# Rank and scatter: the first eight tile loads issued whole in place of two halves

## The chip, the cores and the metric

The kernel runs on one core of a Trainium2 chip. The metric is the time of one execution on the device in microseconds, lower being better. The core has five engines with instruction streams of their own: PE (TensorE), DVE (VectorE), ACT (ScalarE), POOL (GpSimd) and SP (SyncE). SP, ACT and POOL issue DMAs, which run on the core's 16 DMA engines. In the profile each issuing engine has a queue of its own: q0 is POOL's, q1 is SP's and q10 is ACT's.

## What is computed

```python
B, N, D = x.shape                      # 8, 2048, 2560, float32
order = np.argsort(scores, axis=1)
ranks = np.argsort(order, axis=1)
out[b_idx, ranks, :] = x
```

Each of the 8 batches has 2048 rows of 2560 floats (10,240 bytes) and one score per row. A row's place in the output is the rank of its score among the 2048 scores of its batch. So 16,384 rows, 168 MB, are read and written once, each at a place that is known only when the scores have been compared.

## The kernel before

A batch is cut into eight groups of 256 rows (`GROUPS`). In a group each of the 128 partitions holds two neighbouring rows, m = 2, so one partition's part of a group is 20,480 contiguous bytes of `x`.

**Ranks (DVE, PE).** For each batch PE spreads the scores to all partitions and DVE counts, column by column, how many scores are smaller (L238). Of batch 0 the groups' ranks come out in four steps (`STEPS`: group 0, 1, 2 to 3, 4 to 7), of the later batches all at once. The ranks are cast to integers in `rank_i` (L276, and L284 for the groups in `THIN`).

**Bulk path (POOL).** `BULK` lists all groups but group 0 of batches 0 to 5, 58 groups in all. Each is loaded into one of eight buffers `x0` to `x7` (`NBUF`) and sent out by two indirect DMAs, the scatters (L422). A scatter takes one of the two rows of each partition, 128 rows of 10,240 bytes, to the places in `rank_i`. Load 0 is issued by SP, loads 1 to 7 by POOL at once behind its set-up. From then on, POOL issues load k + 4 before it scatters group k, once the scatters of group k - 4 have landed (`LAG`). Before the scatters of group k, POOL waits for the whole of load k and for the group's ranks.

**How a load is cut.** `load` (L126) issues one DMA for a group, or, for the groups whose number is in `HALVED`, one DMA per row of a partition. A half has 128 pieces of 10,240 bytes, a whole load 128 pieces of 20,480. `HALVED` is `range(8)`: the first load of each of the eight buffers. `loaded` counts 16 semaphore steps per DMA, so the wait asks for both halves.

**Row copies (SP, ACT).** Group 0 of batches 0 to 5 (`DIRECT`) does not pass through SBUF. SP copies its first 128 rows and ACT the other 128 straight from HBM to HBM, one DMA of 10,240 bytes per row, in loops that load 16 offsets at a time (L390 to L402). They start a batch when DVE has written its byte offsets into `rows_i` (L324). In group 4 of batches 1 to 7 (`THIN`), the scatters skip partitions 48 to 51 (their ranks are pushed out of bounds by `hole`, L284), and those eight rows go as row copies too (L376), by SP for the first, third, fifth and seventh of these groups and by ACT for the others. SP thus issues 800 row copies, ACT 792. Each is split into 16 pieces of 640 bytes, one for each DMA engine.

**End.** SP and ACT wait for all their row copies, SP for the last scatters of all buffers.

Of the kernel before, what the change touches and what calls it, by code (L numbers as in the profile page):

```python
# [40 lines left out]
def kernel(  # L41
# [25 lines left out]
    THIN = [(b, 4) for b in range(1, B)]  # L67
    HOLES = range(48, 48 + 4)

    HALVED = range(8)  # L70

    STEPS = [(0, 1), (1, 2), (2, 4), (4, 8)]

# [28 lines left out]
    with tc.tile_critical(no_gpsimd_drain=True):  # L102
# [17 lines left out]
        def load(line, k, sem):  # L120
            b, g = BULK[k]
            r, m = GROUPS[g]
            rows = x[b, r:r + P * m, :].rearrange("(p j) d -> p (j d)", j=m)
            for j in range(m if k in HALVED else 1):
                part = slice(j * D, (j + 1) * D) if k in HALVED else slice(0, m * D)
                line.eng.dma_start(  # L126
                    out=xb[k % NBUF][:, part], in_=rows[:, part]
                ).then_inc(sem, 16)
                if k:
                    n_load[k % NBUF] += 1  # L130
# [3 lines left out]
        load(sp, 0, s_first)  # L134
        loaded = {0: (s_first, 16 * (2 if 0 in HALVED else 1))}

# [343 lines left out]
```

## Time and profile before

| What | Value |
|---|---|
| Median of 9 runs | 782.57 us (781.41 to 784.08) |
| Profiled execution, time | 783.25 us |
| Profiled execution, span from first to last instruction | 781.5 us |
| DVE busy | 400.1 us (51%) |
| POOL busy | 150.1 us (19%) |
| PE busy | 36.7 us (5%) |
| HBM read, written | 168.41 MB, 168.35 MB (431 GB/s over the span) |
| POOL's loads (L126) | 64: 50 whole, 14 halves, mean 562 ns |
| POOL's scatters (L422) | 116, mean 969 ns |

A span line counts what an engine executes, a DMA issue on POOL included. The DMA share is the mean busy share of the 16 DMA engines; the records of overlapping packets can bring it a little over 1. In a timeline line the first two numbers are the start and the duration in us, then come the engine (SPq and ACTq are the issuing sequencers of SP and ACT), the line, the operation, what is written and read, how many were merged, and in brackets the idle time before it with what ended it. In a line of waits there are the total in us, the number of waits and the longest. In a line of a stretch, the window and its length are followed by busy time and count on PE, PE's weight loads, DVE, ACT and POOL, then the granted PE clock, the DMA share and GB/s. In a line of a DMA queue there are packets, MB and the share of the 16 engines' span.

The trace also has a record of every DMA packet: its queue, size, start and duration. One packet is one contiguous piece that one DMA engine moves; the 4-byte packets are completion signals.

### The profile page before, as it was taken

How to read it: one execution, taken by the hardware profiler on the slowest of the kernel's cores; microseconds unless marked ns; L12 is line 12 of the kernel's file. 1: busy time of each engine (PE TensorE's matmuls, PEld its weight loads, DVE VectorE, ACT ScalarE, POOL GpSimd, SP SyncE). 2: the span in 40 equal slices, each digit the busy share in tenths (PEclk: the TensorE clock that was granted, in tenths of full speed). 3: DMA queues.
4: the chain of work that ended last, by engine and by line, in shares of the span. 5: the costliest groups of instructions: out<-in, count | busy, mean ns of one | idle time of the engine just before them, and what ended most of it. 6: DMA issues, size and time to landing. Idle time of an engine off the chain costs nothing.

```text
span 781.5 us, 8177 instructions
## 1 busy us (share of the span) xinstructions
PE 36.7 (5%) x170; PEld 31.0 (4%) x170; DVE 400.1 (51%) x825; ACT 0.0 (0%) x1; POOL 150.1 (19%) x189
## 2 busy tenths in 40 slices
PE   4000020020020020120000000000000000000000
PEld 4000010010010010120000000000000000000000
DVE  5999979979979979889999200000000000000000
ACT  0000000000000000000000000000000000000000
POOL 4113122212121212112211211121212121220100
PEclk9655555555555555555555555555555555555555
DMA  8999999999999999999999999999999999999995
GB/s 359 419 421 419 422 415 423 417 421 417 424 416 422 417 424 417 421 419 421 419 423 418 421 421 424 417 421 419 423 421 420 421 423 419 419 422 420 418 415 68
DMA packets 77186, 320.15 MB, mean 410 GB/s; under 512 B 28448, under 2 KB 53920, under 8 KB 53920
## 3 DMA queue, kind: packets, MB, share of 16 engines
q0 software_dynamic: 25920, 300.90, 90.5%
q1 hardware_dynamic: 25904, 10.93, 5.5%
q10 hardware_dynamic: 25344, 8.16, 4.6%
q14 instruction: 17, 0.14, 0.0%
q8 instruction: 1, 0.02, 0.0%
HBM read 168.41 MB, written 168.35 MB: 431 GB/s over the span
## 4 chain that ended last, share of the span: by engine, by line
DMA 44%; DVE 25%; another core or an unknown queue 14%; POOL 5%; issue 5%; PE 2%; POOLq 0%; SPq 0%
DMA out_dram<-x,rank_i 38%; DVE trash L238 23%; DMA x<-in_x_dram 6%; POOL out_dram L422 4%; PE ps_all L196 1%; DVE s_all L339 1%; POOL x L126 1%; DMA s_in<-in_scores_dram 0%; PE ps_row L298 0%; PE ps_col L175 0%; POOLq L446 0%; DVE rank_i L276 0%; DVE rank L270 0%; DVE rank L264 0%
## 5 line engine op out<-in xcount | busy, mean ns | idle before, releaser
L238 DVE TENSOR_SCALAR_CACHE_REDUCE trash<-s_all,s_col 128x1792 bf16<-128x1792 f32 (+7 forms) x240 | 315.2, 1349 | 4.6
L422 POOL DMA_INDIRECT out_dram<-x,rank_i x116 | 112.4, 969 | 142.4 <-DMA x<-in_x_dram 36.4
L126 POOL DMA_DIRECT2D x<-in_x_dram x64 | 35.8, 562 | 445.6 <-DMA out_dram<-x,rank_i 425.5
L238 DVE SCALAR_TENSOR_TENSOR trash<-s_all,s_col,mask 128x256 bf16<-128x256 f32 x128 | 61.6, 482 | 0.0
L196 PE MATMUL ps_all<-ident,s_col 128*128 128x128 f32 x128 | 29.1, 420 | 3.1 <-DVE s_all L339 2.8
L196 PEld LDWEIGHTS ps_all<-ident,s_col 128*128 128x128 f32 x128 | 27.1, 228 | 4.3 <-DVE s_all L339 3.3
L298 PE MATMUL ps_row<-ident,rank 128*1 128x128 f32 x26 | 7.9, 405 | 392.3 <-DVE rank_i L284 334.8
L339 DVE COPY s_all<-ps_all 128x512 f32<-128x512 f32 x32 | 20.2, 685 | 1.7 <-PE ps_all L196 1.4
L238 DVE DVE_READ_ACCUMULATOR trash<-s_all,s_col 128x1 f32 x240 | 20.0, 83 | 0.0
L298 PEld LDWEIGHTS ps_row<-ident,rank 128*1 128x1 f32 x26 | 2.0, 98 | 396.4 <-DVE rank_i L284 337.6
L238 DVE DVE_READ_ACCUMULATOR trash<-s_all,s_col,mask 128x1 f32 x128 | 10.7, 84 | 0.0
L309 DVE TENSOR_SCALAR thin_i<-ps_row 1x8 int32<-1x8 f32 x7 | 1.1, 153 | 18.5 <-PE ps_row L298 18.5
L324 DVE TENSOR_SCALAR rows_i<-ps_row 1x256 int32<-1x256 f32 x6 | 2.5, 411 | 4.1 <-PE ps_row L298 4.1
L183 DVE COPY s_col<-ps_col 128x128 f32<-128x128 f32 x1 | 0.3, 293 | 4.6 <-PE ps_col L175 4.6
L276 DVE CAST rank_i<-rank 128x16 int32<-128x16 f32 (+3 forms) x11 | 2.1, 193 | 0.4
L175 PE MATMUL ps_col<-ident,s_in 8*128 8x8 f32 x16 | 2.1, 262 | 3.7 <-DMA s_in<-in_scores_dram 3.7
L175 PEld LDWEIGHTS ps_col<-ident,s_in 8*128 8x128 f32 x16 | 2.0, 210 | 3.7 <-DMA s_in<-in_scores_dram 3.7
L270 DVE TENSOR_TENSOR rank<-rank,acc 128x16 f32<-128x16 f32 (+3 forms) x11 | 1.9, 171 | 0.4
L264 DVE TENSOR_TENSOR rank<-acc,acc 128x16 f32<-128x16 f32 (+3 forms) x11 | 1.9, 170 | 0.4
L284 DVE TENSOR_SCALAR rank_i<-rank,hole 128x2 int32<-128x2 f32 x7 | 1.6, 229 | 0.2
L156 POOL TENSOR_SCALAR_AFFINE_SELECT mask<-mask 128x256 f32<-128x256 f32 x2 | 0.8, 401 | 0.0
L168 DVE MEMSET acc<- 128x128 f32 x1 | 0.2, 165 | 1.1 <-SPq L102 1.1
(10 smaller groups left out, 1.8 us busy)
## 6 DMA issues: line engine op xcount, KB each, us to landing
x<-in_x_dram POOLq DMA_DIRECT2D x50, 2560.0 KB
x<-in_x_dram POOLq DMA_DIRECT2D x14, 1280.0 KB
out_dram<-in_x_dram SPq DMA_DIRECT2D x800, 10.0 KB
out_dram<-in_x_dram ACTq DMA_DIRECT2D x792, 10.0 KB
x<-in_x_dram SPq DMA_DIRECT2D x2, 1280.0 KB, 9.0
out_dram<-x,rank_i POOLq DMA_INDIRECT x116, 48.5
s_in<-in_scores_dram SPq DMA_DIRECT2D x1, 64.0 KB
```

The lines of the kernel that those rows point to most:

```text
L126: line.eng.dma_start(out=xb[k % NBUF][:, part], in_=rows[:, part]).then_inc(sem, 16)
L175: nc.tensor.transpose(out=ps_col[:, B * c:B * (c + 1)], in_=s_in[:, r + j:r + m * P:m], identity=ident[:B, :B],)
L196: nc.tensor.transpose(out=ps_all[:, P * c:P * (c + 1)], in_=s_col[:, c, b:b + 1].to_broadcast([P, P]), identity=ident[:],)
L238: do(out=trash[i][:, :P * (hi_c - lo_c)], in0=s_all[:, P * lo_c:P * hi_c], accum_out=acc[i][:, col:col + 1], **how,)
L264: nc.vector.tensor_tensor(out=rank[:, cols], in0=acc[0][:, cols], in1=acc[1][:, cols], op=OP.add)
L270: nc.vector.tensor_tensor(out=rank[:, cols], in0=rank[:, cols], in1=acc[2][:, cols], op=OP.add)
L276: nc.vector.tensor_copy(out=rank_i[:, cols], in_=rank[:, cols])
L284: nc.vector.tensor_scalar(out=rank_i[:, cols], in0=rank[:, cols], scalar1=hole[:], scalar2=None, op0=OP.add,)
L298: nc.tensor.transpose(out=ps_row[:1, P * j:P * (j + 1)], in_=rank[:, col:col + 1], identity=ident[:],)
L324: nc.vector.tensor_scalar(out=rows_i[b][:].rearrange("o (p j) -> o p j", p=P), in0=ps_row[:1, :WIDE].rearrange("o (j p) -> o p j", p=P), s ...
L339: nc.vector.tensor_copy(out=s_all[:, 512 * q:512 * (q + 1)], in_=ps_all[:, 512 * q:512 * (q + 1)],)
L422: nc.gpsimd.indirect_dma_start(out=out_flat, out_offset=bass.IndirectOffsetOnAxis(ap=rank_i[:, col:col + 1], axis=0), in_=xb[k % NBUF][:, ...
```

## The change

`HALVED` becomes empty. The first load of each of the eight buffers is issued as one DMA of 2,560 KB with 128 pieces of 20,480 bytes, as the other 50 loads already are. SP issues one DMA less, POOL seven less; the waits on these loads count 16 in place of 32. On POOL and SP the order of everything else stays, and the instructions of PE, DVE and ACT are the same.

```diff
     THIN = [(b, 4) for b in range(1, B)]
     HOLES = range(48, 48 + 4)
 
-    HALVED = range(8)
+    HALVED = range(0)
 
     STEPS = [(0, 1), (1, 2), (2, 4), (4, 8)]
```

The function that reads it:

```python
for j in range(m if k in HALVED else 1):
    part = slice(j * D, (j + 1) * D) if k in HALVED else slice(0, m * D)
    line.eng.dma_start(
        out=xb[k % NBUF][:, part], in_=rows[:, part]
    ).then_inc(sem, 16)
```

## The prediction

> **What bounds the kernel now.** I read the row of DMA shares first. Then the stretches, the waits of SP and POOL, the first issues, and last the tail.
>
> ```profile
> DMA  8999999999999999999999999999999999999995
> q0 software_dynamic: 25920, 300.90, 90.5%
> q1 hardware_dynamic: 25904, 10.93, 5.5%
> q10 hardware_dynamic: 25344, 8.16, 4.6%
> ...
> SPq L390 <- DVE rows_i L324: 15.6, 1, 15.6
> ```
>
> The 16 DMA engines are full in 38 of 40 slices. q0 (what POOL issues: tile loads and scatters) takes 90.5% of them. q1 and q10 carry the row copies of SP and ACT. So an issue or a semaphore matters only if it leaves the engines empty or reorders the end.
>
> ```profile
> 1.50 0.83 SPq L126 DMA_DIRECT2D x<-in_x_dram  x2
> 2.69 7.53 POOL L126 DMA_DIRECT2D x<-in_x_dram  x14
> 25.21 1.00 POOL L422 DMA_INDIRECT out_dram<-x,rank_i  x1 [15.00 <-DVE rank_i L276]
> ```
>
> These are all issues of the loads that the edit touches (start, duration). POOL then waits 15.0 us for a rank, SP 15.6 us for the row offsets of batch 0.
>
> ```profile
> 10.00:20.00 10.00, 3.15 (x16) 3.07 (x16) 9.11 (x16) 0.00 (x0) 0.21 (x1) 1.00 1.01 429
> 23.60:54.80 31.20, 0.00 (x0) 0.00 (x0) 30.60 (x71) 0.00 (x0) 5.82 (x6) 0.51 1.03 419
> 54.80:80.50 25.70, 0.00 (x0) 0.00 (x0) 25.32 (x49) 0.00 (x0) 9.44 (x11) 0.50 1.02 420
> 740.00:760.00 20.00, 0.00 (x0) 0.00 (x0) 0.00 (x0) 0.00 (x0) 0.00 (x0) 0.50 1.03 415
> 764.00:770.00 6.00, 0.00 (x0) 0.00 (x0) 0.00 (x0) 0.00 (x0) 0.00 (x0) 0.50 1.05 100
> ```
>
> The last two columns are DMA share and GB/s. There is no gap to win up to 760 us. The tail is the one poor stretch: 764 to 770 is busy at 100 GB/s. In the records of single DMA packets, q0's last packet ends at 769.7 us, q10's at 774.9 and q1's at 777.1. So row copies end the kernel, after the scatters.
>
> ```profile
> 754.07 5.17 ACTq L376 DMA_DIRECT2D out_dram<-in_x_dram  x8
> 755.85 11.47 SPq L376 DMA_DIRECT2D out_dram<-in_x_dram  x16
> ```
>
> SP issues its last row copies until 767.3 us, ACT until 759.2. Whatever delays the row copies is paid behind these lines.
>
> **The change part by part.** *Issues.* SP has one issue less (0.83 / 2 = 0.42 us). POOL has seven less: 7.53 / 14 = 0.54 us each, 3.8 us. Both then wait as before (15.0 and 15.6 us), which hides the gain; without that cover it would be 3.8 us. Nothing is moved past anything else, no wait is added, and the wait for a buffer still asks for its whole tile.
>
> Nor do the engines starve earlier. x0 reaches all 16 engines by 3.4 us and lasts until q0's first packet at 6.8 us, by the packet records. Its packets hold the same bytes in the same order.
>
> The Trainium skill, "DMA: Bandwidth & Descriptors", section "Anatomy of one DMA", fits one DMA as about 2.0 us fixed plus its bytes. Paid one after the other, eight DMAs less would be an estimated 16 us; the share of 1.01 from 10 to 20 us speaks against it.
>
> *Packets.* A half load moves packets of 10240 B, one per partition, a whole load packets of 20480 B. Mean duration by the packet records is 0.386 us for 10240 B and 0.762 us for 20480 B (300 to 700 us). Two halves cost 0.772, so 0.010 us is saved per partition. Seven POOL loads are 7 x 8 = 56 partitions per engine: 0.56 us. The eighth load, x0, is all start-up (0.427 us per packet), and I give it nothing. Seven completion packets of 0.009 us add 0.06 us. Sum: **-0.6 us** on every engine, bounds 0 and -0.7.
>
> *Row copies.* Each is 16 packets of 640 B, one per engine, with a completion packet behind each (0.032 + 0.009 = 0.041 us of one engine). I counted packets per engine by stretch, taking the two row queues as a mean:
> - 23.6 us (first row copy) to 54.7 (last half-load packet): 74.7 q0 packets, 34.4 row copies, 0.46 per packet.
> - 54.7 to 80.4 (scatters alone): 63.0 and 24.6, 0.39.
> - 80.4 to 160: 145.3 (a third of them 20480 B) and 79.8, 0.55.
> - 160 to 740: 0.564. 740 to 760 (scatters alone): 0.569.
>
> So a row ring with work gets about 0.565 copies through per q0 packet, whatever that packet's size. Halving the number of packets in the first stretch halves what it can carry: 37.3 x 0.565 = 21.1. From 82 to 86 us, all 20480 B, the ratio was lower, 0.48; that would give 17.9.
>
> In before that stretch was not at this limit but at the issue's. SP's issues there take 0.52 us with 0.22 between them and 2.5 us more after each 16 (the offsets are loaded again): 16 in 14.3 us, 1.1 per us, 34 in 31 us.
>
> After therefore leaves 34.4 - 21.1 = 13.3 copies per queue behind. Issued copies not yet moved go from about 5 to 18 in each ring. Before stands at 32 from 500 us on, so no issue is blocked. The engine time that the two queues don't use, 26.6 x 0.041 = 1.1 us, goes to the loads, so they end at 54.7 - 0.6 - 1.1 = 53.0 us.
>
> Then the rows catch up. Scatters alone can carry 63.0 x 0.565 = 35.6 copies, and before moved 24.6: 11.0 to spare, 2.3 left behind. From 80.4 to 160: 145.3 x 0.565 = 82.1 against 79.8, again 2.3 to spare. I take **0 to 1** copy per queue as left at 160 us, after which there is no slack. Bulk work gives back nearly all of its 1.1 us here, because the late copies use it.
>
> Bounds: 0 (all caught up) and 16.5 (lower ratio, nothing caught up). I stay near 0 because the spare is larger than the debt in rows of this same trace.
>
> *Price of a copy left behind.* With the scatters nearly gone (764 to 768 us), each row queue moves 2.85 copies per us. One more per queue is 1 / 2.85 = 0.35 us of tail, less 2 x 0.041 that the bulk gained: 0.27 us. One copy: **+0.3 us**.
>
> The Trainium skill, same page, section "Queues, rings and completion order", says that an engine takes turns between its queues packet by packet, a packet being some 9 to 17 descriptors. The turns agree with the rows. But if a copy's two packets went in one turn, the ratio would be 1 instead of the 0.565 measured, the first stretch would carry 37 and nothing would fall behind; the sum would be -0.6.
>
> **Sum.** -0.6 + 0.3 = -0.3 us. The profiled execution took 783.25 us (span 781.5 and 1.75 around it), so 782.95. It stands 0.68 above the median of 782.57, so about **782.3** for the median. A measurement of this kernel tells some 0.2% (1.6 us) from no change, and this is well inside.
>
> **Rivals.** *Slower: the row copies never catch up.* Place: 54.7 to 80.4 us. The 0.39 there need not be lack of issued work. SP's issues last 0.8 to 1.0 us at 66 to 78 us although only 2 to 4 copies per ring are outstanding on average. If one late engine, or the queue itself, holds them back there, the 11.0 spare does not exist. Then 13.3 - 2.3 = 11 stay behind: 11 x 0.27 - 0.6 = +2.4 us, 785.0. With 16.5 it is +3.9, 786.5. It decides from about 8 copies (8 x 0.27 - 0.6 = 1.6). For it: copies end the kernel, and nothing after 160 us has slack. Against it: 740 to 760 us has the same scatters alone and 0.569.
>
> *Faster: a descriptor costs the slowest engine more than the mean.* The completions of one scatter spread over 1.9 us at 68 us and over 7.2 us at the end (763.0 to 770.2). So one engine runs late, and it sets the last scatter. The scatters leave out 56 rows of four partitions; were all on that engine, 56 x 0.387 = 21.7 us were taken off it. Its handicap would be about 28 us in all. Spread over its 1437 data packets of q0, 56 packets less are 3.9% or 1.1 us. With the 0.6 that is -1.7 us, 780.9. Against it: the packet durations scarcely vary (0.385 to 0.388 in nearly every stretch).
>
> *The engines empty at the start* because whole loads are generated later: POOL's first issue took 0.71 us, the others about 0.53, and the later whole loads take 0.57. A delay of that size is covered by x0, so it is 0 here, and I give it no chance of its own.
>
> **How the numbers follow.** Catching up: 0.42, time 782.3, own range 781.0 to 784.0 (runs of before went from 781.4 to 784.1). Never catching up: 0.36, around 785. Slow engine relieved: 0.22, around 781. The range goes from 780.3 (the fast case less half a microsecond of scatter) to 785.9 (between the two prices of the slow case). Faster 0.22, within 0.2% 0.42, slower 0.36.
>
> **What would show it.** q0 down to 25920 - 7 x 144 = 24912 packets and POOL's L126 to 57. POOL's first loads done at about 6.5 us. About 21 row copies per queue moved when the first whole loads end near 53 us, against 33 and 36, and the gap nearly gone by 80 us. SP's last issue within a microsecond of 767.3, and q1's end likewise of 777.1. I am wrong if at 160 us the row queues are still over 8 copies behind, if the tail past q0's last packet is longer than 7.4 us by more than a microsecond, or if the loads leave the engines idle before 20 us.

## The result and the profile after

After takes 784.5 us (median of 21 runs, 783.72 to 792.14; all but one at or below 785.01) against 782.56 us (63 runs, 781.36 to 784.08): 1.0029 times as long, interval 1.0022 to 1.0036. That is slower by 1.9 us, clear of the 0.2% that I had set as the limit.

The page after, its row of DMA shares and its queues:

```profile
DMA  8999999999999999999999999999999999999995
q0 software_dynamic: 24912, 300.90, 90.3%
q1 hardware_dynamic: 25760, 10.93, 5.8%
q10 hardware_dynamic: 25344, 8.16, 4.3%
```

The edit did what it says: q0 has 25920 - 7 x 144 = 24912 packets and the same bytes. The engines are as full as before. The issues after, from the timelines of POOL, ACT and SP:

```profile
2.68 3.87 POOL L126 DMA_DIRECT2D x<-in_x_dram  x7
25.41 1.00 POOL L422 DMA_INDIRECT out_dram<-x,rank_i  x1 [18.87 <-DVE rank_i L276]
...
756.99 5.25 ACTq L376 DMA_DIRECT2D out_dram<-in_x_dram  x8
...
757.12 10.99 SPq L376 DMA_DIRECT2D out_dram<-in_x_dram  x16
```

POOL is done with the loads at 6.6 us and waits 18.9 us in place of 15.0: the saved issues are all given to that wait. ACT's last row copies are issued until 762.2 us in place of 759.2, SP's until 768.1 in place of 767.3. The end of after in stretches (last columns: DMA share, GB/s):

```profile
740.00:760.00 20.00, 0.00 (x0) 0.00 (x0) 0.00 (x0) 0.00 (x0) 0.00 (x0) 0.50 1.03 417
764.00:770.00 6.00, 0.00 (x0) 0.00 (x0) 0.00 (x0) 0.00 (x0) 0.00 (x0) 0.50 1.05 91
770.00:776.00 6.00, 0.00 (x0) 0.00 (x0) 0.00 (x0) 0.00 (x0) 0.00 (x0) 0.50 0.38 19
```

From 740 to 760 us the two are alike (415 GB/s in before). Then after moves 91 GB/s where before had 100, and the engines are still 38% busy from 770 to 776 us. The same last stretch of before:

```profile
770.00:776.00 6.00, 0.00 (x0) 0.00 (x0) 0.00 (x0) 0.00 (x0) 0.00 (x0) 0.50 0.32 17
```

So the whole loss lies behind the scatters, in the row copies. The rest of this text counts them in the packet records: how many rows the two row queues together have moved by a given time. The counts of every profiled execution, in us and rows:

```
kernel (first loads)           rows moved by          last packet    this
                           54    80   160    740     q0   row copy   execution
before (0-7 in halves)   67.0 117.6 277.7 1473.8   769.7    777.1    783.25
before, second profile   71.8 128.0 286.3 1481.8   770.5    776.0    782.13
after (all whole)        42.9 110.9 274.8 1471.2   769.5    778.2    784.29
after, second profile    42.6 111.0 276.1 1471.6   770.3    779.0    785.13
only load 0 whole        71.1 124.7 284.8 1480.2   770.3    776.8    782.91
loads 0-2 whole          71.0 119.2 280.6 1476.8   770.5    777.2    783.37
loads 3-7 whole          42.6 111.3 276.4 1473.0   769.2    777.9    784.00
loads 1-7 whole          42.4 111.1 275.8 1471.5   769.7    778.4    784.53
8-15 in halves instead   42.4 110.7 287.0 1485.4   770.4    775.3    781.39
row copies from 37 us    30.9  69.9 230.5 1428.3   767.9    787.6    791.85
row copies from 61 us     0.0  14.1 170.2 1369.6   766.3    813.5    817.09
first 24 in halves       71.0 128.0 298.8 1514.1   770.6    770.9    778.12
first 32 in halves       72.4 126.7 297.6 1530.6   770.8    766.6    775.21
all 58 in halves         71.6 125.2 294.0 1592.0   771.9    736.8    777.61
```

### The profile page after: what moved, and what is told of

Read it like the earlier page. It is cut to its first block, busy times and chain, and to the rows that moved or that the text cites. A ratio compares the mean times of both kernels' runs of the same rounds, so it can differ in the third digit from the quotient of the medians.

```text
span 782.6 us, 8169 instructions
## 1 busy us (share of the span) xinstructions
PE 36.7 (5%) x170; PEld 31.0 (4%) x170; DVE 400.0 (51%) x825; ACT 0.0 (0%) x1; POOL 146.6 (19%) x182
## 3 DMA queue, kind: packets, MB, share of 16 engines
q0 software_dynamic: 24912, 300.90, 90.3%
## 4 chain that ended last, share of the span: by engine, by line
DMA 50%; another core or an unknown queue 19%; DVE 13%; POOL 7%; issue 6%; PE 1%; POOLq 0%; SPq 0%
DMA out_dram<-x,rank_i 43%; DVE trash L238 12%; DMA x<-in_x_dram 6%; POOL out_dram L422 5%; POOL x L126 1%; PE ps_all L196 0%; DVE s_all L339 0%; DMA s_in<-in_scores_dram 0%; PE ps_col L175 0%; POOLq L446 0%; DVE rank_i L276 0%; DVE rank L270 0%; DVE rank L264 0%; PE ps_row L298 0%
## 5 line engine op out<-in xcount | busy, mean ns | idle before, releaser
L126 POOL DMA_DIRECT2D x<-in_x_dram x57 | 32.1, 563 | 446.0 <-DMA out_dram<-x,rank_i 404.0
```

Source lines behind the costliest of these rows:

```text
L126: line.eng.dma_start(out=xb[k % NBUF][:, part], in_=rows[:, part]).then_inc(sem, 16)
```

## The experiments

Each was timed in five rounds beside before on the same chip; ratios are to before. A kernel's debt is the number of row copies by which it lies behind before at the same time. The row-debt theory says that whole loads make the kernel slower only by this debt: rows that are late stay late, and end the kernel later.

### Which loads count

`e1_x0_whole`:

```diff
-    HALVED = range(8)
+    HALVED = range(1, 8)
```

> Only load 0 (SP's) is issued whole, loads 1 to 7 stay in halves. Row-debt theory (whole loads slow the row copies only while these run, from 23.6 us on): load 0 has landed by then, so 782.6 us, as before. Start theory (the engines fill later at the start, all 16 at 4.2 us in place of 3.4): most of the +1.9 us, about 784. Equal price for each whole load: +0.24 us, 782.8.

Measured 782.99 us, ratio 1.0015 (1.0006 to 1.0024). Row copies at 54 us are as in before, so the debt theory held there, but the time is 1.1 us up. Its one profiled execution (782.91) ends 0.8 us after that of before's second profile. The engines were all at work from 4.0 us, in before from 3.3. Whether this small loss is the start's I can't tell: the second profile of after also has load 0 whole, and its scores' first packet came at 2.01 us, as in before.

`e2_3to7_whole`:

```diff
-    HALVED = range(8)
+    HALVED = range(3)
```

> Loads 0 to 2 in halves, 3 to 7 whole. Row-debt theory: loads 1 and 2 are gone by the first row copy (23.6 us), so loads 3 to 7 carry the whole effect: about 784.3 us, and the row copies of a queue are some 11 to 13 behind before at 54 us. Start theory: 782.6. Equal price for each whole load: 5/8 of 1.9, 783.8.

Measured 784.98 us, ratio 1.0042 (1.0029 to 1.0056), with 42.6 rows at 54 us against 71.8 in the second profile of before: the debt and the loss of after, out of the five loads that run beside row copies.

`e3_0to2_whole`:

```diff
-    HALVED = range(8)
+    HALVED = range(3, 8)
```

> Loads 0 to 2 whole, 3 to 7 in halves. Row-debt theory: 782.6 us or a shade less (0.2 us of packets saved), with the row copies as in before at 54 us. Start theory: about 784.5. Equal price for each whole load: 3/8 of 1.9, 783.3.

Measured 783.48 us, ratio 1.0020 (1.0011 to 1.0030); the debt theory had said no change. At 54 us it has its 71.0 rows; at 80 us it is 9 behind the second profile of before, and 8 of these it lost in between, where no load runs. SP's issues last 1.05 us on average from 72 to 78 us, against 0.72 in the second profile of before. The first profile of before lost rows in the same place, with 0.97. So this stretch varies from one profiled execution to the next, and why it does stays open. Chance in one execution does not explain the times, though: the medians of `e1_x0_whole` (11 runs) and `e3_0to2_whole` (10 runs) are 1.1 and 1.6 us above before, with both intervals above 1. In the profile of `e3_0to2_whole` the loss goes with late rows (5.0 behind the second profile of before at 740 us, 1.2 us longer), but the row-debt theory gave no reason for rows to be late there. The two small losses also do not add up with the 3.1 us of `e2_3to7_whole` to the loss of after (1.9 us in the main comparison, 2.9 on the chip of the second profiles). Their cause is open.

`e6_0_halved`:

```diff
-    HALVED = range(8)
+    HALVED = range(1)
```

> Only load 0 in halves, the other seven first loads whole. Row-debt theory alone: as after, 784.5 us. With a share for the start (first packet of the scores at 2.0 us where load 0 is in halves, 2.25 where it is whole): 0.3 to 1.2 us less than after. If the halves of loads 1 and 2 matter: not the same as the kernel with loads 0 to 2 in halves, which took 785.0.

Measured 784.92 us, ratio 1.0035 (1.0021 to 1.0048), as after on the same chip (785.17). What load 0 in halves saves beside seven whole loads is within the noise.

### Is the profile of before a typical one?

`b2_before_again` is the kernel before, `a2_after_again` the kernel after, unchanged.

> The kernel before, unchanged, for a second profile. If the profiled execution of before was no typical one (SP's row copies held up between 35 and 55 us: 33.1 done on SP and 36.8 on ACT at 55 us), this one shows some 71 row copies done at 54 us and 1480 at 740 us, as the kernel with only load 0 whole had, in place of 67 and 1474. If it was typical, 67 and 1474 again. Time 782.5 us by both.

> The kernel after, unchanged, for a second profile and its time beside the others. Row-debt theory: again some 43 row copies done at 54 us and 1471 at 740 us, 784.5 us. If the debt is chance, the counts differ by more than 5.

Before: 782.13 us, ratio 0.9997 (0.9988 to 1.0006), with 71.8 rows at 54 us, 128.0 at 80 and 1481.8 at 740. This execution is the median of the 11 runs here (0.4 us below the median of the main comparison), and I take it as the typical one from here on. The profile I had predicted from was 10 rows short of it at 80 us. After: 785.17 us, ratio 1.0037 (1.0024 to 1.0051), and its counts agree with its first profile within 1.3 rows at each of the four times. The ends of the two, before first:

```profile
764.00:770.00 6.00, 0.00 (x0) 0.00 (x0) 0.00 (x0) 0.00 (x0) 0.00 (x0) 0.50 1.01 110
770.00:776.00 6.00, 0.00 (x0) 0.00 (x0) 0.00 (x0) 0.00 (x0) 0.00 (x0) 0.50 0.16 11
```

```profile
764.00:770.00 6.00, 0.00 (x0) 0.00 (x0) 0.00 (x0) 0.00 (x0) 0.00 (x0) 0.50 1.06 100
770.00:776.00 6.00, 0.00 (x0) 0.00 (x0) 0.00 (x0) 0.00 (x0) 0.00 (x0) 0.50 0.41 22
```

From 770 to 776 us the typical before is busy at 16%, after at 41%. With the scatters' last packet at 770.5 and 770.3 us, the row copies' last one is at 776.0 and 779.0. These 3.0 us are the difference of the two executions (782.13 and 785.13).

### Is it the debt, or the form of the loads?

`d1_rows_late` keeps all halves and makes the row copies start later; `d2_rows_later` has 4 in place of 2:

```diff
+        for line in (sp, act):
+            line.after(dve, t_bulk[0, 2])
         for b in DIRECT:
```

> All eight first loads in halves as before, but SP and ACT begin their row copies only when the ranks of groups 2 and 3 of batch 0 are there (about 37 us in place of 19.5). Row-debt theory: some 35 row copies fewer at 54 us than the 72 of before, more than the 29 that whole loads cost; then the same catching up, 10 to 16 behind at 740 us, and at 0.28 us a copy 785 to 786.5 us, though no load is changed. If whole loads cost through something else than late row copies: 782.2 us.

> As the one before, with the row copies beginning at the last ranks of batch 0 (about 61 us). Row-debt theory: some 85 row copies behind at 61 us; a ring with more issued work moves up to 1.35 copies per us and queue, but SP and ACT issue 1.1, so little of it is caught up until the ranks of batch 1 come: 45 to 75 behind at 740 us, and at 0.28 us a copy 795 to 803 us. If a late copy costs what I took in the prediction (0.27 us for one on each queue, 0.13 a copy): 788 to 792 us.

Measured 792.18 us (1.0134, 1.0119 to 1.0149) and 816.97 us (1.0444, 1.0431 to 1.0458). Late row copies alone make the kernel slower, with every load as in before. But I had both sizes wrong. I had expected them to catch up as in after; they did not: 41 rows behind at 54 us, 58 at 80 and 54 at 740. In after the issue goes on and the copies wait in the rings, so a ring can run at its full 0.565 copies per q0 packet afterwards. Here the issue itself is late, and it is too slow to make up for it. The last issues of the first of the two, SP's timeline:

```profile
754.52 19.80 SPq L404 DMA_DIRECT2D out_dram<-in_x_dram  x25
775.19 11.26 SPq L376 DMA_DIRECT2D out_dram<-in_x_dram  x16
```

SP still issues at 786.4 us, over 18 us after the last scatter packet (767.9). The second of the two costs 25.2 us more (profiled executions) for 58.7 rows more, 0.43 us a row: there the end goes at the pace of the issues (16 in 14.3 us on each of two queues, or 0.45 us a row). So these two runs show that late row copies cost time, but not at the price that they have in after.

`c1_8to15_halved` leaves the first eight loads whole, as after, and halves the next eight:

```diff
-    HALVED = range(8)
+    HALVED = range(8, 16)
```

> The first eight loads whole as after, loads 8 to 15 in halves in their place: as many halves as before, moved from 2-55 us to 80-190 us. Row-debt theory: 43 row copies at 54 us as after, then up to 1.1 per us and queue in place of 1.02 while halves run, so the debt is gone by 190 us and the row copies are some 5 to 10 ahead of before at 740 us: 779.5 to 782 us. If the form of the first loads counts by itself: 784.5 to 785 us.

Measured 780.68 us, ratio 0.9976 (0.9964 to 0.9987). At 54 and 80 us it has the counts of after (42.4 and 110.7), at 160 us those of before (287.0), and it ends faster than both kernels. With the same whole first loads, the loss is gone once the rows have been made up. So it is not the form of the first loads in itself that costs the 1.9 us, but the rows that it leaves behind.

### Getting ahead of the scatters

`e4_all_halved`, `e5_32_halved` and `e7_24_halved`:

```diff
-    HALVED = range(8)
+    HALVED = range(58)   # range(32), range(24)
```

> All 58 loads in halves. Row-debt theory (a row copy that is late at the end costs tail): each row ring then carries 1.35 copies per us, more than the 1.1 that SP and ACT issue, so the row copies are done near 745 us, ahead of the scatters, and nothing is left past q0's last packet. Price: 50 more split loads x 0.08 us = 4.0 us of packets on every engine. The tail of before holds 12.9 us of idle engine time (mean over the engines); if some 5 of it stay, 782.6 + 4.0 - 8 = 778.6 us, between 776 and 782. If late row copies aren't what costs time, 782.6 + 4.0 = 786.6 us.

> The first 32 of 58 loads in halves. Row-debt theory: about 0.05 to 0.06 more row copies per us and queue than before from 110 us to about 480, some 20 per queue ahead there, so that few are left when the scatters end; packets cost 24 x 0.08 = 1.9 us. Between before and all in halves, or better than both: 776.5 to 779.5 us. If only the complete absence of a row tail counts: 781 or more.

> The first 24 loads in halves. Row-debt theory: 8 pairs less to pay than with 32 (0.08 us each, 0.7 us in all), but 12 to 16 row copies fewer done at 740 us, which cost only as far as they end after the scatters: 775.2 to 777.5 us.

Measured 777.88 us (0.9955, 0.9941 to 0.9968), 775.66 us (0.9917, 0.9904 to 0.9931) and 778.54 us (0.9958, 0.9946 to 0.9971). With 32 halves the end looks like this:

```profile
764.00:770.00 6.00, 0.00 (x0) 0.00 (x0) 0.00 (x0) 0.00 (x0) 0.00 (x0) 0.50 0.54 228
770.00:776.00 6.00, 0.00 (x0) 0.00 (x0) 0.00 (x0) 0.00 (x0) 0.00 (x0) 0.54 0.02 8
```

In 764 to 770 us it moves 228 GB/s with the engines half idle, where the second profile of before moved 110 with them full: what is left there are mostly scatters. Its row copies end at 766.6 us, before the last scatter at 770.8. The version with 32 is the best that was run: 6.6 us less than before on the same chip.

Only the time with 58 lies in the range that I had given. With 32 it is below it (776.5 to 779.5), with 24 above it (775.2 to 777.5). All 58 halves bring the row copies' end to 736.8 us, much earlier than is of use, and cost 2.2 us more than 32 by the medians, 3.0 by the ratios. With 24 the last row packet comes 0.3 us after the last scatter packet, and the kernel is some 3 us slower than with 32. Neither difference lies in the packets alone: q0's last packet comes 1.1 us later with 58 than with 32, and 0.2 us earlier with 24. What ends these three kernels is POOL's `drain` behind its last scatter (L446). Its lines with 32, 58 and 24 halves, and last in the second profile of before (durations in ns, then the start in us):

```profile
L446 POOLq DRAIN  x1: 32527/32527/32527, 740.1 to 740.1; - x1
L446 POOLq DRAIN  x1: 32254/32254/32254, 742.7 to 742.7; - x1
L446 POOLq DRAIN  x1: 37078/37078/37078, 738.4 to 738.4; - x1
L446 POOLq DRAIN  x1: 37605/37605/37605, 737.2 to 737.2; - x1
```

It ends at 772.6 us with 32, at 775.0 with 58 and at 775.5 with 24. SP's last wait is for POOL in all three. These 2.4 and 2.9 us are the differences of the profiled executions (775.21, 777.61 and 778.12). In before it ends at 774.8 us, while the row copies still run, so it costs nothing there. Why it takes 37 us in most kernels here and 32 in two was not found. So a price per further split load can't be read from these times, and once the row copies are out of the way it is this wait that bounds the kernel.

## Why the prediction failed, step by step

**Right: the issues.** POOL's seven issues less (3.87 us in place of 7.53) went into its wait for the rank, as said, and the engines stayed full: a DMA share of 0.97 from 5 to 10 us and 1.00 from 10 to 20, in before 1.01 in both. All 16 engines were at work at 3.9 us in place of 3.3, a delay that the prediction had put at nothing; whether it is part of the small losses above stays open.

**Wrong in size: the packets, "-0.6 us".** The 20480 B packets took 0.761 us only until the first row copy at 23.6 us. From there to 54.6 us, where two thirds of the first whole loads move, they took 0.775 us in one profile of after and 0.781 in the other, while two halves take 0.772: no saving beside row copies. I had taken the 0.762 from 300 to 700 us. q0's last packet came 0.2 us earlier in each of the two pairs of profiles.

**Right: how whole loads hold up the row copies.** I expected 21.1 copies per queue by the end of the whole loads and 0.565 per q0 packet; it was 22.0, and 0.568 (23.6 to 54.6 us). About 17 to 20 issued copies waited in each ring at 54 us, where I had 18. The debt at 54 us was 14.6 copies per queue against the typical before; I had 13.3.

**Wrong: "the rows catch up", and "0 to 1 copy per queue" left.** The ring did its part: 34.3 copies from 54.6 to 80.4 us at 0.561 per q0 packet, where I had 35.6. The spare was wrong. I took the 24.6 copies of before's profile as its pace and so saw 11.0 to spare; the second profile moved 27.3 in the same stretch, and more before it. Against that one 8.5 copies per queue are left at 80 us, 5.1 at 160 and 5.1 at 740. The profile that I had was itself of an execution with late row copies, and with 783.25 us a slow one of before's runs: 8 of the 63 took longer. I had noted the 0.68 us above the median and moved the sum by it, but had not asked what in that execution was late. At 0.22 to 0.29 us a row (below), the 1.9 us of the main comparison stand for an estimated 3 to 4 copies per queue. Against the first profile of before, after is only 1.3 copies per queue behind at 740 us, which is nearly what I said, and 1.0 us longer.

**Wrong in size: the price of a copy left behind, "0.27 us".** Between the second profiles 10.2 rows (5.1 per queue) go with 3.0 us: 0.29 us a row, or 0.59 for one on each queue, twice my price. A straight line through all nine profiles that end on row copies and keep the issue of before (the first nine of the table; rows at 740 us against time) gives 0.22 us a row, or 0.43. I had divided by the mean rate of the 16 engines from 764 to 768 us. The end is set by the engines that finish last. Of the 16 completions of before's last scatter, 14 come by 765.3 us and the other two at 768.9 and 770.2. The last six completions of SP's row copies follow each other at 0.19 us in both second profiles, and a 640 B packet of q1 takes 0.21 to 0.22 us on average past 770 us there, next to 0.03 beside scatters. That shows part of the price; a row's full 0.29 us is not accounted for packet by packet.

**The rivals.** The slower one had the right place (54.7 to 80.4 us), sign and size (785.0 for 784.5 measured, and 785.17 beside before on another chip) but not the right course. Rows did catch up, by two thirds of the debt, and 5 copies per queue were enough where I had asked for 8, since each costs more. The relief of a slow engine did not show: q0's end moved by 0.2 us, not by 1.7. Late engines there are, and two of them, as the completions above show.

**The ring's turns.** Put one behind the other wherever one ends as another starts, the packets fall into 16 sequences, as many as there are engines (745 to 752 us, second profile of before). In these, one packet of q0 is followed by one of q1 and one of q10: 92% of all steps go in this order from 740 to 760 us in the second profile of before, 95 and 98% from 30 to 54 us in the two of after, with 10240 B and 20480 B packets alike. A copy's data packet and completion packet take separate turns, and so does q0's own completion, one for eight pieces. That gives (9 / 8) / 2 = 0.56 copies per q0 piece, the ratio that was measured in the long stretches where the rings had work (0.56 to 0.57). So the turns are there, but a turn here is one such packet, not the 9 to 17 descriptors that the prediction quotes.

## What to carry to other kernels

Where queues share the DMA engines packet by packet, the packet size of the big stream sets the pace of the small one; look at which of them ends last, and give the small one its turns early, by smaller packets in the big one, until it no longer ends last. The best version here has it done 4 us ahead of the scatters; the one in which both end within 0.3 us is slower, and so is the one in which it is done 35 us ahead. Then look at what ends the kernel next, here a `drain`. A debt in such a stream is made good only while issued work is waiting and the engines have turns to spare; once both queues run at their limit, it stays to the end. And a spare read from one profiled execution is worth a second profile before a forecast rests on it, above all if that execution is not near the median.

## What the runs showed of the hardware

- A 640 B packet from HBM to HBM holds an engine for 0.032 us while scatters run (740 to 760 us). In the tails of before and after, the packets of SP's row copies take 0.20 to 0.22 us on average from 770 to 776 us. From 764 to 770 us the engines are full there (1.01 to 1.06) and move only 91 to 110 GB/s. The end of the scatters alone does not do it: with 24 halves, SP's last 12 packets past 770 us take 0.032 us each. What does was not found.
- The last completion of SP's row copies came 2.9 us after their last packet (780.0 and 777.1 us in before). With 32 halves, where a scatter ends last, its completion came 0.4 us after the last packet (771.2 and 770.8 us). The 2.9 us do not belong to every row copy: the last one of SP came 0.3 us after its packet with 32 halves (766.9 and 766.6) and 0.4 us with row copies from 61 us (813.9 and 813.5).
- SP's issue of a row copy takes 0.53 us on average from 19 to 55 us and from 740 us on (second profile of before), but 0.72 us between 72 and 78 us, and 1.05 with loads 0 to 2 whole, where three to four copies wait in each ring. It differs from execution to execution; the cause was not found.
- POOL's `drain` behind the last scatter takes 37.1 to 37.6 us in 12 of the 14 profiles, and 32.3 to 32.5 with 32 and 58 halves; the cause was not found.
